# Attention scores in runs of three units and six PSUM banks instead of two units and four, in a two-layer hybrid decoder kernel

## Chip, cores, metric

One Trainium2 chip (trn2), all eight cores, one batch element on each. The metric is device time in microseconds (us) of the slowest core. A run has one of two states: fast, or slow, in which the cores of one die or of both show a lower granted TensorE clock. Only fast runs are compared. Because one die is sometimes a little disturbed within a fast run too (clock 0.99 instead of 0.998), I use a second, finer measure throughout: the mean span of the four cores of a die, taken over all dies of the timed runs whose four clocks are 0.9965 or more (my threshold; such a die counts also where the other die of its run was slow). These "undisturbed dies" of one kernel scatter by only 1.0 to 2.0 us (standard deviation), so differences of 3 us can be read from 8 to 16 of them.

## The reference

```python
for l in range(DEPTH):                                    # 2 layers
    h = h + 0.5 * g1 * swiglu(modulate(rmsnorm(h)), ffn1)  # feed-forward, width 2816
    proj = modulate(rmsnorm(h)) @ w_in                     # 1024 -> 2560: u, v, q, k, v_b
    out_a = spatial_gating(u, v, ...)
    out_b = dilated_mixture(q, k, v_b)                     # 8 heads of 64; windows (128,1), (512,4), (2048,16)
    h = h + g2 * (concat(out_a, out_b) @ w_out)
    h = h + 0.5 * g3 * swiglu(modulate(rmsnorm(h)), ffn2)
return rmsnorm(h, final_g)
# ... x is (8, 4096, 1024); a branch of the mixture works on blocks of 128 queries
# against the block before and the block itself, masked; the three branches are
# combined by their softmax denominators
```

## The kernel before

The program is recorded as tasks; a scheduler in Python gives each engine a fixed order from estimated durations and gives out the eight PSUM banks. The TensorE works through a main line (feed-forward, projections) and fits in the attention wherever its turn comes. The attention is done for two heads ("a pair") at a time: 4 pairs, 3 dilations, 8 units, so 96 units for each half of the sequence, 384 in the two layers. A unit is two blocks of queries for two heads.

```python
def scores(self, r, us, pos):               # one chain on TensorE, here for two units
    ins, banks = [], []
    for u in us:
        sb = Bank(2)                        # a unit's scores take two banks, one for each head
        banks.append(sb)
        ...
        for off, dims, ko, c, n in todo:    # 128 or 256 columns
            for h in range(2):              # head h: partitions 64*h to 64*h+63, half of the array's rows
                ...
                ins.append((lambda e, ...: e.matmul(bank(sb, h)[:, c:c + n], lhsT=ka, rhs=qa, ...),
                            [bq, bkb], 37.0 if n == 128 else 55.0))
    ins[0] = ins[0][:2] + (110.0,)
    ins[-1] = ins[-1][:2] + (110.0,)
    G.chain(ins, banks, "qk", pos=pos, extra=self.pvs[-2:-1])
    return banks

# ... then, for each unit:
#   ScalarE  exp of both banks into bf16 (gives the two banks back)
#   VectorE  times the mask
#   TensorE  up to 8 matmuls by V into one bank
#   ScalarE or VectorE  the bank added to the accumulator

def normalise(self, p, pos):                # after the last unit of a pair
    for c in range(4):
        ...                                 # ScalarE: two logarithms of 64 rows, one exp(-x) of 128
        # activation(func=AF.Ln), activation(func=AF.Ln), activation(func=AF.Exp, scale=-1.0)
        # POOL: accumulator times the result; DMA out

# feed-forward, for each of 22 column blocks and each tile of 512 tokens:
#   TensorE  8 matmuls "gate" into one bank, 8 "up" into another
#   ScalarE  tanh(gate / 2);  VectorE  (tanh + 1) * gate, gives the gate bank back
#   VectorE  times up, gives the up bank back

# the scheduler, before it takes a task for TensorE that needs n new banks:
if (t.pos > hp + 4000.0 or n > 1) and ... and sum(x <= now for x in pfree["ps"]) < self.RESERVE + n:   # RESERVE = 2
    ...                                     # not now
```

The softmax here doesn't subtract the row's maximum and nothing guards it: scores larger than these inputs give would overflow.

Of the kernel before, what the change touches and what calls it, by code (L numbers as in the profile page):

```python
# [68 lines left out]
class Graph:  # L69
# [30 lines left out]
    def _new(self, name, pos):  # L100
        t = Task()
        t.id = len(self.tasks)
        t.name = name
        t.pos = pos
        t.cur = self.M if pos is None else pos
        t.L = None
        t.wl = None
        t.main = False
        t.due = None
        t.part = None  # L110
        t.soft = ()
        t.mate = None
        t.banks, t.new = [], []
        t.nbytes, t.dma = 0, False
        t.eng = None
        t.tok = None
        t.succ = []
        self.tasks.append(t)
        return t
# [93 lines left out]

    POOLS = {"ps": 8}
    RESERVE = 2

    def schedule(self, bw=270.0, dlat=2300.0, dmargin=3000.0, cmargin=250.0, backlog=9000.0):
        pend = {e: [] for e in ENG}
# [2 lines left out]
        pfree = {p: [0.0] * n for p, n in self.POOLS.items()}  # L221
# [3 lines left out]
        order = []  # L225
        table = [None]
        pipe = [0.0]
        port = [0.0]
        for t in self.tasks:
            t.ndep = len(t.deps)  # L230
# [52 lines left out]
        def pick(e, now):  # L283

            av = avail[e]
            nxt = pend[e][0][0] if pend[e] else 1e18
            if e == "pe":
                best, bk = None, None
                while head[0] < len(mains) - 1 and mains[head[0]].eng is not None:
                    head[0] += 1  # L290
                hp = mains[head[0]].pos
                for t in av:
                    if best is not None and (t.mready <= now, -t.pos) <= bk:
                        continue
                    if t.new:
                        i, f = find_places(t.new, now)
                        if i is None:
                            nxt = min(nxt, f)
                            continue
                        n = sum(b.n for b in t.new)  # L300
                        if (t.pos > hp + 4000.0 or n > 1) and not (t.mate and t.mate.eng) and sum(x <= now for x in pfree["ps"]) < self.RESERVE + n:
                            nxt = min(nxt, max(now + 50.0, sorted(pfree["ps"])[self.RESERVE + n - 1]))
                            continue
                    best, bk = t, (t.mready <= now, -t.pos)
                return best, nxt
            best, bk = None, None
            while head[0] < len(mains) - 1 and mains[head[0]].eng is not None:
                head[0] += 1
            hp = mains[head[0]].pos
            for t in av:  # L310
                if t.new:
                    i, f = find_places(t.new, now)
                    if i is None:
                        nxt = min(nxt, f)
                        continue
                    if t.dma and (t.L > hp + 16000.0 or sum(x <= now for x in pfree[t.new[0].pool]) < 3):
                        nxt = min(nxt, now + 300.0)
                        continue
                if e != t.opts[0][0] and t.L > hp + 2500.0:
                    nxt = min(nxt, now + 300.0)  # L320
                    continue
                if not t.dma and t.mready > t.ready:
                    m = t.mready + max(0.0, min(6000.0, 0.5 * (t.L - hp - 5000.0)))
                    if m > now and t.L > hp + (m - now) + 1000.0:
                        nxt = min(nxt, max(m, now + 200.0))
                        continue
                if t.dma:
                    far = t.L - hp
                    bl = backlog if far < 12000.0 or now < 100000.0 else 5000.0 if far < 40000.0 else 2500.0
                    if pipe[0] - now > bl:  # L330
                        nxt = min(nxt, max(pipe[0] - bl, now + 50.0) if bl == backlog else now + 200.0)
                        continue
                    if pipe[0] - now > 3000.0 and any(x.dma and x.eng is None and x.L < t.L and not x.new
                                                      for x in avail["pool" if e == "sp" else "sp"]):
                        nxt = min(nxt, now + 200.0)
                        continue
                k = t.L
                if e == "dve" and port[0] > now and any(o[0] == e and o[3] == "x" for o in t.opts):
                    k += 2.0 * (port[0] - now)
                if e == "act":  # L340
                    f = next(o[3] for o in t.opts if o[0] == e)
                    if f is not None and table[0] not in TABLES[f]:
                        k += 3000.0
                if best is None or k < bk:
                    best, bk = t, k
            return best, nxt
# [4 lines left out]
        while done < total:  # L351
            cand = sorted(ENG, key=lambda e: (when[e], EI[e]))
            e = cand[0]
            now = when[e]
# [3 lines left out]
            p = pend[e]  # L358
            while p and p[0][0] <= now:
                t = heapq.heappop(p)[2]  # L360
# [3 lines left out]
            t, nxt = pick(e, now)  # L364
# [29 lines left out]
                t.ins[0] = (t.ins[0][0], t.ins[0][1] | prev) + t.ins[0][2:]  # L394
            free[e] = st + dur
            t.start, t.dur = st, dur
            if t.dma:
                pipe[0] = max(pipe[0], st + dur) + t.nbytes / bw
                t.end = pipe[0] + dlat
                t.late = max(t.end, t.mready + dur + 2000.0) + dmargin  # L400
            else:
                t.end = st + dur + LAT[e]
                t.late = max(t.end, t.mready + o[2] + LAT[e] if e != "pe" else 0.0)
# [177 lines left out]
def build_nc():  # L581
# [34 lines left out]
    with ExitStack() as st:  # L616
        arena = st.enter_context(nc.sbuf_tensor("arena", [128, AW], F32))
        ps = st.enter_context(nc.psum_tensor("ps", [128, 8, 512], F32))
# [51 lines left out]
        def steps(lo, size, n):  # L670
            return [lo + size * i for i in range(n)]
# [587 lines left out]

        BACK = {1: 128, 4: 512, 16: 2048}  # L1260

        class Attn:
            def __init__(self, half, p0, p1):
                self.half = half
                z = ACT[2]

                def at(n):
                    nonlocal z
                    z += n
                    return z - n  # L1270
                self.q = Ring([at(4096)], [128, SB], BF16, "q")
                self.k = Ring([at(8192 if half else 4096)], [128, 2 * SB if half else SB], BF16, "k")
                if half:
                    self.v = {1: Ring([at(6528)], [128, 17, 192], BF16, "v1"), 4: Ring([at(7680)], [128, 20, 192], BF16, "v4"),
                              16: Ring([at(12288)], [128, 32, 192], BF16, "v16")}
                else:
                    vv = Ring(steps(at(12288), 6144, 2), [128, 16, 192], BF16, "v")
                    self.v = {1: vv, 4: vv, 16: vv}
                self.acc0 = at(16384)
                self.pT = Ring(steps(at(6144), 2048, 3), [128, 2, 2, 2, 128], BF16, "pT")  # L1280
                self.ob = Ring(steps(at(2048), 1024, 2), [128, T], BF16, "ob")
                self.hi = z
                self.pvs = []
                units = [(p, r, u) for p in range(4) for r in (1, 4, 16) for u in range(8)]
                step = (p1 - p0) / (len(units) + 2)
                for n, (p, r, u) in enumerate(units):
                    pos = p0 + step * n
                    if r == 1 and u == 0:
                        self.start_pair(p, pos)
                    if u == 0:  # L1290
                        self.load_v(p, r, pos)
                    if u % 2 == 0:
                        banks = self.scores(r, (u, u + 1), pos)
                    self.unit(p, r, u, pos, step, banks[u % 2])
                    if r == 16 and u == 7:
                        self.normalise(p, pos + step)

# [47 lines left out]
                rho = 2 * u + b  # L1345
                return rho * 8, [[128, 16], [1, 8]], rho, bool(half), rho, 16 * half + rho

            def scores(self, r, us, pos):



# [1 line left out]
                q, k, bq, bkb = self.qa, self.ka, self.bq, self.bk  # L1353
                kb = SB if self.half else 0
                ins, banks = [], []
                for u in us:
                    sb = Bank(2)
                    banks.append(sb)
                    b0, b1 = self.blk(r, u, 0), self.blk(r, u, 1)
# [11 lines left out]
                    for off, dims, ko, c, n in todo:  # L1371
                        for h in range(2):
# [1 line left out]
                            ka = bass.AP(k.tensor, k.offset + h * 64 * k.ap[0][0] + kb + ko, [[k.ap[0][0], 64], [r, 128]])  # L1374
                            ins.append((lambda e, qa=qa, ka=ka, h=h, c=c, n=n, sb=sb: e.matmul(  # L1375
                                bank(sb, h)[:, c:c + n], lhsT=ka, rhs=qa, start=True, stop=True), [bq, bkb],
                                37.0 if n == 128 else 55.0))
                ins[0] = ins[0][:2] + (110.0,)
                ins[-1] = ins[-1][:2] + (110.0,)
                G.chain(ins, banks, "qk", pos=pos, extra=self.pvs[-2:-1])  # L1380
                return banks

# [343 lines left out]
```

## Time and profile before

| | before |
|---|---|
| first three timed runs | 4849.52, 5211.05, 5432.37 us (one fast, two slow) |
| span in the profile, slowest core | 4871.8 us |
| undisturbed dies, three chips | 4828.4, 4827.5, 4827.1 us |
| TensorE busy | 98% |
| runs of score matmuls | 192 |

The profile has these parts used below: the busy share of each engine; the chain of work that ended last; the waits (who waited for whom, us in total, times, longest); and the instructions in order of time. In the latter a row reads: start in us, duration in us, engine, source line, operation, out<-in, shape, count, and in brackets the idle time ahead of it with what ended it. Durations of matmuls are modelled and overlap; differences of starts are what to rely on. In the kernel before, L1375 are the score matmuls, L1409 those by V, L1002 gate and up, L1393 the exponential of scores, L1008 the tanh, L1436 and L1438 the logarithms, L1440 the exponential of the normalisation. In the changed kernel the same lines are L1392, L1426, L1017, L1410, L1023, L1453, L1455 and L1457.

### The profile page before, as it was taken

The page shows a single profiled execution, that of the slowest core. Times are in us where ns is not written, and L with a number is a line of the kernel's source. Part 1 is how long each engine was busy: PE and PEld are TensorE (multiplying, and loading weights), DVE is VectorE, ACT ScalarE, POOL GpSimd, SP SyncE. Part 2 cuts the span into 40 slices and gives each one's busy share as a digit, 9 for nine tenths or more (in the row PEclk, how much of TensorE's full clock was granted, in tenths as well). Part 3 has the DMA queues.
Part 4 walks back from the last instruction along what each step waited for, and adds up shares of the span by engine and source line. Part 5 has one row for each costly group of instructions (what it writes and reads, how often), then busy time and mean ns, then how long its engine had stood idle before and what let it go on. Part 6 is the DMA issues. An engine that isn't in the chain of part 4 may idle for free.

```text
span 4871.8 us, 74168 instructions; the slowest of 8 cores (4820.7 to 4871.8 us)
## 1 busy us (share of the span) xinstructions
PE 4789.6 (98%) x25859; PEld 2257.4 (46%) x25859; DVE 2461.2 (51%) x4088; ACT 2035.0 (42%) x3024; POOL 973.5 (20%) x949
## 2 busy tenths in 40 slices
PE   6999999999999999999999999999999999999998
PEld 2444445444445554444444444444444455544443
DVE  6452566473655473655233326645537544525433
ACT  5112576452755352512211127645537444525311
POOL 0001551212531111300100026312235100122101
PEclk9999999999999999999999999999999999999999
DMA  8888676777575768755721466756665644473314
GB/s 240 169 191 230 166 204 159 191 206 218 172 209 150 200 192 240 218 147 165 249 66 39 120 200 163 208 155 184 149 190 164 185 148 140 123 248 124 136 42 157
DMA packets 370033, 834.80 MB, mean 171 GB/s; under 512 B 148961, under 2 KB 182113, under 8 KB 363234
## 3 DMA queue, kind: packets, MB, share of 16 engines
q1 hardware_dynamic: 352338, 741.56, 49.4%
q0 software_dynamic: 17328, 88.49, 12.1%
q8 instruction: 213, 3.49, 0.3%
q14 instruction: 154, 1.26, 0.1%
HBM read 741.20 MB, written 234.88 MB: 200 GB/s over the span
## 4 chain that ended last, share of the span: by engine, by line
PE 92%; ACT 2%; DMA 2%; DVE 2%; issue 1%; POOL 0%; SPq 0%; DVEq 0%; ACTq 0%; POOLq 0%
PE ps L1002 48%; PE ps L1030 25%; PE ps L1141 9%; PE ps L1467 5%; PE ps L1409 3%; PE ps L1375 2%; DMA arena<-xP 1%; DMA arena<-hS 0%; DVE arena L1206 0%; DVE arena L948 0%; POOL arena L1182 0%; DMA arena<-ada_w 0%; ACT arena L1184 0%; DMA arena<-wdS 0%; PE ps L1234 0%
## 5 line engine op out<-in xcount | busy, mean ns | idle before, releaser
L1002 PE MATMUL ps<-arena 128*128 128x512 bf16 x11264 | 2511.5, 381 | 32.6 <-DMA arena<-wgu 25.0
L1002 PEld LDWEIGHTS ps<-arena 128*128 128x128 bf16 x11264 | 1083.9, 98 | 1312.0 <-issue 86.4
L1030 PE MATMUL ps<-arena 128*128 128x512 bf16 x5632 | 1242.7, 382 | 1.1 <-DMA arena<-wdS 1.1
L1008 ACT ACTIVATE arena<-ps 128x512 f32<-128x512 f32 x704 | 419.7, 597 | 1283.7 <-PE ps L1002 1279.9
L1010 DVE SCALAR_TENSOR_TENSOR arena<-arena,ps 128x512 f32<-128x512 f32 x704 | 481.4, 685 | 771.9 <-ACT arena L1008 770.7
L1030 PEld LDWEIGHTS ps<-arena 128*128 128x128 bf16 x5632 | 550.7, 98 | 665.6 <-issue 47.9
L926 POOL TENSOR_TENSOR arena<-arena 128x512 f32<-128x512 f32 (+2 forms) x351 | 414.2, 1180 | 1218.4 <-ACT arena L919 1116.3
L1034 DVE SCALAR_TENSOR_TENSOR arena<-ps,arena 128x512 f32<-128x512 f32 x256 | 192.1, 751 | 908.3 <-PE ps L1030 899.9
L1015 DVE TENSOR_TENSOR arena<-ps,arena 128x512 bf16<-128x512 f32 x704 | 485.0, 690 | 216.6 <-PE ps L1002 193.3
L1141 PE MATMUL ps<-arena 128*128 128x512 bf16 x2560 | 577.1, 385 | 9.0 <-ACT arena L1225 5.8
L919 ACT ACTIVATE arena<-arena 128x512 bf16<-128x512 f32 x424 | 250.9, 625 | 709.1 <-DVE arena L1034 379.3
L1393 ACT ACTIVATE arena<-ps 128x1024 bf16<-128x1024 f32 (+1 forms) x384 | 344.9, 950 | 308.3 <-PE ps L1375 307.6
L1141 PEld LDWEIGHTS ps<-arena 128*128 128x128 bf16 x2560 | 251.0, 99 | 314.7 <-issue 52.0
L1396 DVE TENSOR_TENSOR arena<-arena 128x1024 bf16<-128x1024 bf16 (+1 forms) x384 | 256.1, 675 | 126.0 <-ACT arena L1393 124.6
L961 ACT ACTIVATE arena<-arena 128x512 bf16<-128x512 f32 x372 | 278.4, 806 | 45.2 <-DVE arena L948 45.1
L1445 POOL TENSOR_TENSOR arena<-arena 64x512 bf16<-64x512 f32 x128 | 163.8, 1280 | 623.1 <-ACT arena L1440 600.0
L948 DVE TENSOR_TENSOR arena<-arena 128x512 f32<-128x512 f32 x384 | 268.3, 747 | 35.0 <-ACT arena L934 32.0
L1467 PE MATMUL ps<-arena 128*128 128x512 bf16 x1024 | 230.1, 386 | 0.0
L1425 DVE TENSOR_TENSOR arena<-ps,arena 128x512 f32<-128x512 f32 x256 | 175.5, 685 | 65.2 <-PE ps L1409 57.5
L1409 PEld LDWEIGHTS ps<-arena 128*128 128x128 bf16 x2736 | 173.6, 98 | 63.4 <-issue 7.1
L1213 POOL TENSOR_TENSOR arena<-arena 128x512 bf16<-128x512 f32 x128 | 167.9, 1320 | 174.8 <-DVE arena L1204 120.2
L1409 PE MATMUL ps<-arena 128*128 128x128 bf16 x2736 | 194.4, 219 | 1.9 <-DVE arena L1010 0.9
(79 smaller groups left out, 2112.7 us busy)
## 6 DMA issues: line engine op xcount, KB each, us to landing
arena<-wguS SPq DMA_DIRECT2D x242, 512.0 KB, 5.7
arena<-hS SPq DMA_DIRECT2D x204, 512.0 KB, 6.8
arena<-wdS SPq DMA_DIRECT2D x128, 704.0 KB, 5.9
arena<-ada_w SPq DMA_DIRECT2D x144, 512.0 KB, 5.9
hS<-arena SPq DMA_DIRECT2D x224, 256.0 KB, 5.8
wguS<-wgu POOLq DMA_DIRECT2D x66, 512.0 KB, 7.8
hS<-arena SPq DMA_DIRECT2D x64, 512.0 KB, 4.3
arena<-xP SPq DMA_DIRECT2D x48, 512.0 KB, 9.0
```

What stands on the lines that cost most here:

```text
L926: f = lambda e, a=a, sq=sq, out=out: e.tensor_tensor(out=out, in0=a, in1=sq, op=ALU.add)
L948: f = lambda e, hk=hk, u=u: e.tensor_tensor(out=u, in0=hk, in1=rs, op=ALU.mult)
L961: ga = act(lambda e, hk=hk, A=A, sh=sh, o=o: e.activation(out=o, in_=hk, func=AF.Identity, scale=A, bias=sh), 725)
L1002: mate = main([(lambda e, kc=kc, half=half, bk=bk, y=y, gu=gu: e.matmul(bank(bk), lhsT=gu[:, half, kc, :], rhs=y[:, kc, :], start=(kc == 0 ...
L1008: G.op([act(lambda e, sg=sg, gb=gb: e.activation(out=smv[sg.i], in_=bank(gb), func=AF.Tanh, scale=0.5), 490, "tanh")], reads=[gb], writes= ...
L1010: G.op([dve(lambda e, sg=sg, gb=gb: e.scalar_tensor_tensor(out=smv[sg.i], in0=smv[sg.i], scalar=1.0, in1=bank(gb), op0=ALU.add, op1=ALU.mu ...
L1015: G.op([dve(lambda e, sg=sg, ub=ub, o=o: e.tensor_tensor(out=o, in0=bank(ub), in1=smv[sg.i], op=ALU.mult), 610)], reads=[ub, sg], writes=[ ...
L1030: main([(lambda e, j=j: e.matmul(bank(bk), lhsT=wd[:, j, :], rhs=a[:, j, :], start=(j == 0), stop=(j == FC - 1)), [bwd, ba[j]], MM) for j ...
L1141: ins.append((lambda e, lhs=lhs, rhs=rhs, kc=kc: e.matmul(bank(bk), lhsT=lhs, rhs=rhs, start=(kc == 0), stop=(kc == KC - 1)), rd + [by[kc] ...
L1393: return e.activation(out=cut(pT, 0), in_=cut(ps[:, :, :], sb.i * 512), func=AF.Exp, scale=0.125)
L1409: return e.matmul(o, lhsT=v[:, vi, h * 64:h * 64 + 128], rhs=pT[:, h, b, pc, :], start=(pc == 0 or not prev), stop=(pc == 1))
L1467: main([(lambda e, kc=kc, m=m, bk=bk: e.matmul(bank(bk), lhsT=w[:, m, kc, :], rhs=mx[:, kc, :], start=(kc == 0), stop=(kc == KC - 1)), [bw ...
```

## The change

The intent is fewer changes between half-row and full-row matmuls: the scores of three units are issued in one run, so that there are 32 runs in a half instead of 48. The cost is that a run takes six of the eight banks.

```diff
-                    if u % 2 == 0:
-                        banks = self.scores(r, (u, u + 1), pos)
-                    self.unit(p, r, u, pos, step, banks[u % 2])
+                    if n % QKG == 0:                                   # QKG = 3
+                        banks = self.scores(units[n:n + QKG], pos)
+                    self.unit(p, r, u, pos, step, banks[n % QKG])
...
-                                37.0 if n == 128 else 55.0))
-                ins[0] = ins[0][:2] + (110.0,)
-                ins[-1] = ins[-1][:2] + (110.0,)
+                                55.0 if n == 256 else 28.0 if r < 16 else 31.0))
+                ins[0] = ins[0][:2] + (ins[0][2] + 109.0,)
+                ins[-1] = ins[-1][:2] + (ins[-1][2] + 109.0,)
...
-  ... sum(x <= now for x in pfree["ps"]) < self.RESERVE + n:
+  ... sum(x <= now for x in pfree["ps"]) < (7 if n == 6 else self.RESERVE + n):
...
+    PFAR, PLEN, PRATE = 1e9, 3000.0, 0.7
+                    if far > self.PFAR and now > 100000.0 and pace[0] - now > self.PLEN:   # never true: PFAR
+                        t.held = True
```

More of the change, by code (lines that the diff above doesn't have):

```diff
@@ L112, in _new @@
         t.mate = None
+        t.held = False
         t.banks, t.new = [], []
@@ L227, in schedule @@
         pipe = [0.0]
+        pace = [0.0]
+        pes = []
         port = [0.0]
@@ L300, in pick @@
                         n = sum(b.n for b in t.new)
-                        if (t.pos > hp + 4000.0 or n > 1) and not (t.mate and t.mate.eng) and sum(x <= now for x in pfree["ps"]) < self.RESERVE + n:
-                            nxt = min(nxt, max(now + 50.0, sorted(pfree["ps"])[self.RESERVE + n - 1]))
+                        if (t.pos > hp + 4000.0 or n > 1) and not (t.mate and t.mate.eng) and sum(x <= now for x in pfree["ps"]) < (7 if n == 6 else self.RESERVE + n):
+                            nxt = min(nxt, max(now + 50.0, sorted(pfree["ps"])[(7 if n == 6 else self.RESERVE + n) - 1]))
                             continue
@@ L331, in pick @@
                         nxt = min(nxt, max(pipe[0] - bl, now + 50.0) if bl == backlog else now + 200.0)
+                        continue
+                    if far > self.PFAR and now > 100000.0 and pace[0] - now > self.PLEN:
+                        t.held = True
+                        nxt = min(nxt, max(pace[0] - self.PLEN, now + 100.0))
                         continue
@@ L396, in schedule @@
             t.start, t.dur = st, dur
+            if e == "pe":
+                pes.append(t)
+            if t.dma and t.held:
+                x = next((x for x in reversed(pes) if x.end + 100.0 <= now), None)
+                if x is not None:
+                    t.deps = t.deps | {x}
             if t.dma:
+                pace[0] = min(max(pace[0], now) + t.nbytes / (bw * self.PRATE), max(now + 8000.0, pipe[0] + t.nbytes / bw))
                 pipe[0] = max(pipe[0], st + dur) + t.nbytes / bw
@@ L1260, in build_nc @@
         BACK = {1: 128, 4: 512, 16: 2048}
+        QKG = 3
         class Attn:
@@ L1346, in blk, with scores @@
                 return rho * 8, [[128, 16], [1, 8]], rho, bool(half), rho, 16 * half + rho
-            def scores(self, r, us, pos):
+            def scores(self, us, pos):
                 q, k, bq, bkb = self.qa, self.ka, self.bq, self.bk
@@ L1355, in scores @@
                 ins, banks = [], []
-                for u in us:
+                for _, r, u in us:
                     sb = Bank(2)
```

## The prediction

> **What bounds the kernel now.** I read the cores first, then the page's busy shares and chain, then the waits of the TensorE, then the TensorE's instructions in order of time inside an attention stage.
>
> The cores, then the page (busy time, and the chain by engine):
>
> ```profile
> core 5: 4871.8 us, clock 0.989
> die 0 (median of its cores): 4824.8 us, clock 0.998
> die 1 (median of its cores): 4864.5 us, clock 0.990
> ```
>
> ```profile
> PE 4789.6 (98%) x25859; PEld 2257.4 (46%) x25859; DVE 2461.2 (51%) x4088; ACT 2035.0 (42%) x3024; POOL 973.5 (20%) x949
> ...
> PE 92%; ACT 2%; DMA 2%; DVE 2%; issue 1%; POOL 0%; SPq 0%; DVEq 0%; ACTq 0%; POOLq 0%
> ```
>
> The profile fell in the fast state (both dies near full clock, 0.8% apart). The TensorE is busy 98% of the span and is 92% of the chain that ended last; the next engine, VectorE, is at 51%. So the span is the sum of what the TensorE streams plus what makes it stand still, and a gain must come out of that sum. The scores are one source line, L1375, two forms of 64-row matmuls (groups by form):
>
> ```profile
> L1375 PE MATMUL ps<-arena 64*128 64x128 bf16 x1792 | 117.9, 225 | 2.7 <-ACT arena L1008 1.4 <-DVE arena L1015 1.2
> L1375 PE MATMUL ps<-arena 64*128 64x256 bf16 x512 | 63.4, 269 | 0.0
> ```
>
> They lost 2.7 us to waits in the whole kernel. What they cost besides is only seen in order of time (start, duration, instructions), here 15 us of the second attention half of layer 0, the TensorE and below it ScalarE and VectorE rows of the same stretch:
>
> ```profile
> 1702.28 1.89 PE L1002 MATMUL ps<-arena 128*128 128x512 bf16 x8
> 1704.10 0.63 PE L1375 MATMUL ps<-arena 64*128 64x128 bf16 x12
> 1704.66 3.63 PE L1002 MATMUL ps<-arena 128*128 128x512 bf16 x16
> 1708.13 1.06 PE L1409 MATMUL ps<-arena 128*128 128x128 bf16 x16
> 1709.02 1.89 PE L1002 MATMUL ps<-arena 128*128 128x512 bf16 x8
> 1710.84 0.63 PE L1375 MATMUL ps<-arena 64*128 64x128 bf16 x12
> ```
>
> ```profile
> 1704.10 0.42 PEld L1375 LDWEIGHTS ps<-arena 64*128 64x128 bf16 x12 [0.42 <-issue]
> ...
> 1704.83 1.94 ACT L1393 ACTIVATE arena<-ps 128x1024 bf16<-128x1024 f32 x2
> ...
> 1705.96 0.69 DVE L1396 TENSOR_TENSOR arena<-arena 128x1024 bf16<-128x1024 bf16 x1 [0.23 <-ACT arena L1393]
> ...
> 1707.35 0.68 DVE L1396 TENSOR_TENSOR arena<-arena 128x1024 bf16<-128x1024 bf16 x1
> ```
>
> Durations here overlap, so only differences of starts count. One cycle serves two units: a run of 12 score matmuls, 16 feed-forward matmuls (L1002), 16 that multiply by V (L1409), 8 feed-forward. The 8 feed-forward matmuls ahead of the scores take 1704.10 - 1702.28 = 1.82 us; where ordinary matmuls follow, the same 8 take 1.73 (mean 1.728 over 32 places, against 1.822 over 101 places with scores behind them). So **going into a run costs 0.094 us**. The note "0.42 <-issue" says that the weight loads of the scores, which elsewhere run ahead of the matmuls, did not start earlier here.
>
> **What the Trainium skill says.** "TensorEngine Tiling (Array Packing)", Key Properties: changing the tiling mode, not just the tile, drains the TensorE. Scores contract over 64 rows and the two heads use the two halves of the array, so each run is entered and left by a mode change; the trace agrees with 0.094 us in. "TensorE: Matmul & The Clock Gate", "Wait — 56ns, not 53.3ns?": warm start to start is N / 2.4 GHz plus about 2.5 ns, 215.7 ns at N = 512. The trace agrees: 1.728 / 8 = 0.216 us. The tiling page, "Gotcha 1: PSUM Pressure": row tiles write different PSUM banks, which is why a unit takes two banks; "PSUM — Partial Sum Buffer", Specifications: there are eight. The change moves a run from four of them to six; no trace of the kernel before can show what six do.
>
> **The cost of leaving.** Start of a run to start of what follows, over runs without a wait: 0.398 us for 8 matmuls of 128 columns (32 runs), 0.648 for 16 of them (32 runs), 0.558 for 12, of which 4 have 256 columns (120 runs). The first two give 0.250 / 8 = 31 ns a matmul and a constant of 0.398 - 8 x 0.03125 = 0.148 us. For the 12, the two heads' streams of 1024 columns at the page's 2.4 GHz are 0.427 us (an estimate), which leaves 0.131. So **leaving costs 0.13 to 0.15 us**, and a run as a whole 0.094 + 0.14 = 0.235.
>
> **The change part by part.**
>
> 1. Runs. 2 layers x 2 halves x 96 units are 384 units: 192 runs of two before, 128 of three after. In the built programs the score matmuls stand in 192 runs (128 of 12, 32 of 8, 32 of 16) and in 128 (80 of 18, the others of 12, 14, 22 and 24). Each program has 2304 score matmuls, 2736 by V, and all others in equal numbers. So 64 runs go: 64 x 0.235 = 15.0 us (14.3 with 0.131, 15.5 with 0.148), and all of it lies on the TensorE, thus on the path.
>
> 2. The scores' estimates in the scheduler, and its rule that a run of six banks starts only when seven of the eight are free. They cost nothing by themselves but decide the order. With two units a run and the old estimates put back into the new file, all five engines' orders come out equal to before, so the third part of the diff, the pacing of far transfers, never acts (its threshold of 1e9 is never reached).
>
> 3. What the order makes of it. Until the first scores of each layer the TensorE's order hardly differs (8 feed-forward matmuls more ahead of them), so the start (89 us until the long feed-forward runs, over 60 of them waits for data) stays. Every run is still followed by at least 8, nearly always 16 feed-forward matmuls or a 22-matmul down chain before the first multiplication by V. After the last multiplication by V of a half, at least 340 matmuls of 512 columns (over 70 us) still stand before the output projection that needs it, in both programs. So attention stays buried in feed-forward work, and nothing waits for its end.
>
> 4. Waits. Six banks must be read out by three exponentials, each 1.94 / 2 = 0.97 us, then three maskings of 0.69. In the cycle above the exponentials would end at 1705.8, 1706.8 and 1707.7, the third masking at about 1708.04 + 0.69 = 1708.7 (the second ended at 1708.04), while the third multiplication by V would start at 1708.13 + 2 x 0.45 = 1709.03: 0.3 us of slack, an estimate from this one cycle. Two banks are left for feed-forward. The first gate chain lasts 1.73 us, and the first exponential gives two banks back about 1.2 us after the run, so the third chain finds one. But the margin is thinner than the 0.5 us of today's second unit. In the four attention stages the TensorE's waits sum to 1.7, 0.5, 1.2 and 1.6 us, 5.0 in all (the first stage, over 440 us):
>
> ```profile
> PE ps L1375 <- ACT arena L1008: 0.7, 1, 0.7
> PE ps L1375 <- DVE arena L1015: 0.5, 1, 0.5
> PE ps L1409 <- DVE arena L1010: 0.5, 1, 0.5
> ```
>
> I expect this to double or to treble: 5 us lost, with 0 to 15 possible.
>
> The sum: -15.0 + 5 = -10 us, 0.2% of the span.
>
> **The rivals.**
>
> Bank starvation: with two free banks, gate and up chains wait for exponentials, or the scores for their seven banks. For it: eight banks in all, and the rule of seven had to be made (the old rule of two in reserve would ask for eight). Against it: ScalarE is busy 229 of 410 us in the first stage and VectorE 251, and the new order keeps 16 or more feed-forward matmuls behind each run. If each of the 128 runs lost 0.5 us, that is +64 us and a net of +49, 1% slower; two waits of 0.5 would be needed in every run for 2%.
>
> No gain per run: if the drain is paid per head pair or per matmul, not per run, longer runs save nothing and the time stays at -0 to +5. Against it: 8 and 16 matmuls differ by 31 ns each, close to the 27 ns that half of 128 columns takes at 2.4 GHz, so little per-matmul cost is left to be hidden there.
>
> Gain hidden by another bound: a DMA or VectorE path sets the end. Against it: the PE share of the chain, and 0.2% is too little to uncover the next bound at 51%. It would leave 0.
>
> More banks, smoother order: fewer chain breaks could also remove today's 5 us of attention waits, for -20. I give this little.
>
> **Range and chances.** The before runs were 4849.52, 5211.05 and 5432.37 us, the latter two over 7% above the first and so slow; the prediction is for a fast run, as only such are compared. 4849.5 - 10 = 4840. The size of the effect is uncertain by -20 to +50, and fast spans differ by chip and die by some 0.5% (4871.8 in the profile with one die at 0.990, 4824.8 for the other die), so 4800 to 4890. Faster by 2% would take 97 us; all that the mode changes cost now is 192 x 0.235 = 45. So faster 0.01, within 2% 0.96, slower 0.03. Where a run falls in the slow state, it lies hundreds of us higher, for both kernels.
>
> **What would show it.** Step 1: 128 runs; 8 feed-forward matmuls ahead of one still take 1.82 us; a run of 18 takes 0.558 + 0.213 = 0.77 us, a run of 24 takes 0.148 + 24 x 0.03125 = 0.90. If 18 take 0.84 (1.5 times 0.558) the per-run cost is wrong. Step 3: starts of the first feed-forward, and the stretch from the last scores to the output projection, as before. Step 4: the TensorE's waits inside the four attention stages sum to 5 to 20 us, on L1409's and L1375's counterparts; over 20, with feed-forward waiting for ScalarE or VectorE, means the bank rival. The prediction is wrong if fast runs of the same rounds differ by over 0.6% (30 us) or the new kernel is the slower.

## The result, and the profile after

Ratios are the mean time of one kernel's fast runs over that of the other's fast runs of the same rounds, so they are not quite the ratios of the medians.

| | before | after |
|---|---|---|
| median of 6 runs, both states | 4915.72 us | 4856.27 us |
| fastest run | 4846.83 us | 4844.41 us |
| ratio of fast runs | | 1.0009 (95%: 0.9989 to 1.0029) |
| undisturbed dies, same chip and rounds (run again later) | 4827.1 us (14 dies) | 4826.3 us (8 dies) |

The time did not move: the medians differ only because more of before's runs were slow, and on undisturbed dies the difference is 0.8 us, where 10 had been forecast.

The cores, the busy shares and the chain of the changed kernel:

```profile
core 5: 4853.0 us, clock 0.993
die 0 (median of its cores): 4826.7 us, clock 0.998
die 1 (median of its cores): 4846.7 us, clock 0.993
```

```profile
PE 4762.0 (98%) x25859; PEld 2254.9 (46%) x25859; DVE 2465.2 (51%) x4088; ACT 2041.4 (42%) x3025; POOL 978.2 (20%) x952
...
PE 93%; ACT 2%; DMA 2%; issue 1%; DVE 1%; POOL 0%; SPq 0%; DVEq 0%; ACTq 0%; POOLq 0%
```

The span of the page is 19 us shorter than before's 4871.8, but that is core 5, on die 1, at clock 0.993 instead of 0.989. Die 0, undisturbed in both, went from 4824.8 to 4826.7. The TensorE is the bound as before.

**An account of the TensorE.** To see where the forecast gain went I summed up the TensorE's rows of the trace after the first 600 us: from each row's start to the next one's, less the wait noted at the next, less 0.2159 us for each matmul of 512 columns and 0.0558 for each of 128. What is left ahead of the scores is the cost of going in (with any standing that no wait names). Means of three undisturbed cores before (1 to 3) and six after, in us:

| term | before | after (second profile) | difference |
|---|---|---|---|
| the runs of scores, start to what follows | 105.0 | 96.6 | -8.4 |
| remainder ahead of runs | 19.0 | 14.4 | -4.6 |
| waits that the trace names | 18.1 | 28.8 | +10.7 |
| remainder elsewhere | 7.2 | 8.9 | +1.7 |
| sum | 149.3 | 148.7 | -0.6 |

So the saving is there, 13.0 us, and waits and unnamed standing take 12.4 of it back. Where? "Losses" below are the named waits around the attention, plus standing of over 0.1 us ahead of a run and named waits within the 12 rows that follow it. They went from 7.7 to 17.3 us a core, and those that fall **at the first run of a pair of heads** from 3.1 to 13.0. That is 0.8 us on average over the 16 pairs (from 0 to 2.3); the other runs lose 4.3 us in all, where it was 4.6 before. Here are two such places, core 1. Before, the TensorE and ScalarE rows:

```profile
788.18 0.62 PE L1375 MATMUL ps<-arena 64*128 64x128 bf16 x12
788.73 5.35 PE L1002 MATMUL ps<-arena 128*128 128x512 bf16 x24
...
787.01 1.28 ACT L1436 ACT_TABLE_LOAD   x1
788.31 0.63 ACT L1436 ACTIVATE arena<-arena 64x512 f32<-64x512 f32 x1
788.95 1.28 ACT L1008 ACT_TABLE_LOAD   x1
790.25 0.60 ACT L1008 ACTIVATE arena<-ps 128x512 f32<-128x512 f32 x1
790.74 1.94 ACT L1393 ACTIVATE arena<-ps 128x1024 bf16<-128x1024 f32 x2
```

And after:

```profile
778.72 21.52 PE L1017 MATMUL ps<-arena 128*128 128x512 bf16 x96
800.37 0.84 PE L1392 MATMUL ps<-arena 64*128 64x128 bf16 x18
801.14 1.90 PE L1017 MATMUL ps<-arena 128*128 128x512 bf16 x8
804.04 1.89 PE L1017 MATMUL ps<-arena 128*128 128x512 bf16 x8 [1.00 <-DVE arena L1025]
...
798.44 1.28 ACT L1453 ACT_TABLE_LOAD   x1
799.74 0.63 ACT L1453 ACTIVATE arena<-arena 64x512 f32<-64x512 f32 x1
800.46 0.63 ACT L1455 ACTIVATE arena<-arena 64x512 f32<-64x512 f32 x1
801.10 1.28 ACT L1023 ACT_TABLE_LOAD   x1
802.40 0.60 ACT L1023 ACTIVATE arena<-ps 128x512 f32<-128x512 f32 x1
802.89 2.85 ACT L1410 ACTIVATE arena<-ps 128x1024 bf16<-128x1024 f32 x3
```

In both, ScalarE is not ready when the scores are: it is in the normalisation of the pair before, with a table load to the logarithm and one back. The exponentials start equally late, 790.74 - 788.18 = 2.56 us after the run's start before and 802.89 - 800.37 = 2.52 after. Before, 24 feed-forward matmuls (three banks) go by without a wait, as a run leaves four banks. There ScalarE is held from 787.01 to 790.25, 3.24 us. After, it is held from 798.44 to 802.40, 3.96 us. The first 8 feed-forward matmuls fit in; the next 8 need a bank that waits for a tanh at 802.40 and then for VectorE (L1025), and the TensorE stands for 1.00 us. The run of 96 matmuls ahead also shows standing that no wait names: 800.37 - 778.72 = 21.65 us, where 96 x 0.2159 and 0.094 for going in make 20.82. (With 1.00 + 0.83 us this is one of the dearer places.)

That is a theory so far: **the six banks leave the TensorE two, and at the start of each pair ScalarE, held up by table loads, gives banks back too late (A)**. Rivals: any burst of three exponentials is too long for two banks, wherever it comes (A2); the scheduler's new estimates made a worse order by themselves; or the saving read from the starts isn't real on the path.

### The profile page after: what moved, and what is told of

Its sections match the earlier page's. It is cut to its first block, busy times and chain, and to the rows that moved or that the text cites. A ratio compares the mean times of both kernels' runs of the same rounds, so it can differ in the third digit from the quotient of the medians.

```text
span 4853.0 us, 74112 instructions; the slowest of 8 cores (4822.7 to 4853.0 us)
## 1 busy us (share of the span) xinstructions
PE 4762.0 (98%) x25859; PEld 2254.9 (46%) x25859; DVE 2465.2 (51%) x4088; ACT 2041.4 (42%) x3025; POOL 978.2 (20%) x952
## 4 chain that ended last, share of the span: by engine, by line
PE 93%; ACT 2%; DMA 2%; issue 1%; DVE 1%; POOL 0%; SPq 0%; DVEq 0%; ACTq 0%; POOLq 0%
PE ps L1017 48%; PE ps L1045 25%; PE ps L1156 10%; PE ps L1484 5%; PE ps L1426 3%; PE ps L1392 2%; DMA arena<-xP 1%; ACT arena L1023 0%; DVE arena L1221 0%; DMA arena<-wguS 0%; POOL arena L1197 0%; DMA arena<-hS 0%; DMA arena<-ada_w 0%; PE ps L1249 0%; ACT L1453 0%
## 5 line engine op out<-in xcount | busy, mean ns | idle before, releaser
L1025 DVE SCALAR_TENSOR_TENSOR arena<-arena,ps 128x512 f32<-128x512 f32 x704 | 482.0, 686 | 803.7 <-ACT arena L1023 802.6
L1413 DVE TENSOR_TENSOR arena<-arena 128x1024 bf16<-128x1024 bf16 (+1 forms) x384 | 255.2, 683 | 97.4 <-ACT arena L1410 95.7
L1442 DVE TENSOR_TENSOR arena<-ps,arena 128x512 f32<-128x512 f32 x256 | 175.9, 687 | 60.3 <-PE ps L1426 53.9
```

The lines of the kernel that those rows point to most:

```text
L1025: G.op([dve(lambda e, sg=sg, gb=gb: e.scalar_tensor_tensor(out=smv[sg.i], in0=smv[sg.i], scalar=1.0, in1=bank(gb), op0=ALU.add, op1=ALU.mu ...
```

## The experiments

Twelve kernels ran, in three groups; the kernels of a group shared chip and runs of before. The accounts (us a core, undisturbed cores of the profile with all records) in one table; the experiments follow.

| kernel | runs | scores and remainder ahead | losses | of them first run of a pair | undisturbed dies | before, same rounds |
|---|---|---|---|---|---|---|
| before | 192 | 124.0 | 7.7 | 3.1 | | 4827 to 4828 |
| changed (e12) | 128 | 111.0 | 17.3 | 13.0 | 4826.3 | 4827.1 |
| e1 two units, new estimates | 192 | 123.9 | 7.6 | 2.4 | 4828.1 | 4828.4 |
| e2 one unit | 344 | 160.7 | 10.2 | (runs merge, not told apart) | 4867.5 | 4828.4 |
| e3 three, no logarithm | 128 | 109.3 | 3.6 | 2.7 | 4810.6 | 4828.4 |
| e4 first run of two | 144 | 113.0 | 12.8 | 6.7 | 4823.2 | 4828.4 |
| e5 two, no logarithm | 192 | 123.1 | 2.5 | 2.0 | 4820.8 | 4827.5 |
| e6 two, six banks | 192 | 124.4 | 15.8 | 7.0 | 4853.9 (fast runs, clock 0.995 up) | 4827.5 |
| e7 runs of 2,2,2,3,... | 144 | 112.4 | 10.2 | 2.8 | 4822.1 | 4827.5 |
| e8 logarithms joined | 128 | 109.7 | 19.8 | 14.8 | 4831.5 | 4827.5 |
| e9 three, after normalisation | 128 | 109.2 | 4.6 | 2.6 | 4810.0 | 4827.1 |
| e10 two, after normalisation | 192 | 123.3 | 3.2 | 2.7 | 4820.6 | 4827.1 |
| e11 rule of eight | 128 | | | | 5613.5 (fast runs) | 4827.1 |

### e1: the new estimates alone

```diff
-        QKG = 3
+        QKG = 2
```

> Two units a run again, but with the scheduler's new estimates for the scores: the part of the change that only reorders. Theory A (the longer runs save about 12 us of mode changes and their six banks bring about 11 us of new TensorE waits): this kernel has the 192 runs and the four banks of before, so its score runs plus entries sum to 123 us as before, its losses in the attention to about 8 us, and its time equals before within 0.1%. Rival (the new estimates alone make the order worse, whatever the banks): 8 to 12 us slower than before, ratio 1.002.

Measured: ratio 1.0016 (0.998 to 1.0052; one of the six runs had a die at clock 0.988), undisturbed dies 4828.1 against 4828.4; 192 runs, losses 7.6. The estimates and the reordering that comes of them are worth nothing either way. That rival falls.

### e2: one unit a run

```diff
-        QKG = 3
+        QKG = 1
```

> One unit a run: the program has 344 runs of scores instead of 192. If going in and out costs 0.22 us a run, as the traces of before and after give (0.094 in, 0.13 out), the score runs and their entries take 152 x 0.22 = 34 us more than before, 157 us in all, and the time is 30 to 36 us longer (ratio 1.006 to 1.0075), less up to 5 us of today's waits, as a run takes two banks only. If the saving per run that I read from the starts is not real on the path, the ratio is 1.000 to 1.002.

Measured: ratio 1.0086 (1.0071 to 1.01), dies 4867.5, 39.1 us above before. The score runs took 126.1 us and the remainder ahead of them 34.6; less before's 124.0 that is 36.7 us for 152 runs, 0.24 us each. The time rose slightly more than the range I gave, by the losses (10.2 instead of 7.7), which I had expected to shrink. So the price of a run is real and lies on the path, in the size that the starts gave.

### e3 and e5: the same orders without the logarithm's table

```diff
-  e.activation(out=rc()[0:64, :], in_=acc[64:128, c, 0, :], func=AF.Ln)
+  e.activation(out=rc()[0:64, :], in_=acc[64:128, c, 0, :], func=AF.Identity, scale=0.015)
```

(and the same for the other half; e5 with two units and the old estimates besides). Their outputs are wrong, which doesn't matter for the times. The scheduler is still told "ln", so no instruction moves; only the table loads around the logarithms go.

> The changed kernel in exactly its order, but the logarithms in the normalisation that ends each pair of heads are replaced by a scaled copy, which needs no other activation table: wrong result on purpose, and no instruction added or moved. Theory A1 (ScalarE is held up at the start of each pair of heads by the table loads of the pair before, 1.28 us each, so the exponentials give the six banks back late): the losses at the first run of a pair fall from 13 us to under 5 us a core, all attention losses from 18 to under 9, and the time is 8 to 12 us below the changed kernel's, so ratio 0.998 against before. Rival A2 (any burst of three exponentials is too long for the two banks that are left): the losses stay at 15 us or more and the time stays.

> The kernel before in exactly its order, with the logarithms of the normalisation replaced by the scaled copy (wrong on purpose), so without their table loads. Theory (longer runs save 12 us; their banks need ScalarE at the start of a pair, which the table loads hold up): the losses fall from 8 to about 3 us a core, so the time is 4 to 6 us below before (ratio 0.999), and the three-unit kernel without logarithms, 17 us below before, stays 11 to 13 us better than this one: the gain of the longer runs without their cost. Rival (the table loads cost both kernels the same 14 us or more, and the longer runs gain nothing even without them): this one is 14 to 17 us below before too.

Measured: e3 ratio 0.9964 (0.9942 to 0.9985), dies 17.8 us below before; e5 ratio 0.9983 (0.9957 to 1.0008), 6.7 us below before. The same place in e3, core 1:

```profile
773.67 20.88 PE L1017 MATMUL ps<-arena 128*128 128x512 bf16 x96
794.48 0.84 PE L1392 MATMUL ps<-arena 64*128 64x128 bf16 x18
795.25 3.63 PE L1017 MATMUL ps<-arena 128*128 128x512 bf16 x16
...
794.65 0.60 ACT L1023 ACTIVATE arena<-ps 128x512 f32<-128x512 f32 x1 [0.91 <-PE ps L1017]
795.42 2.86 ACT L1410 ACTIVATE arena<-ps 128x1024 bf16<-128x1024 f32 x3 [0.18 <-PE ps L1392]
```

ScalarE is idle when the scores come, the three exponentials start 0.94 us after the run's start, and 16 feed-forward matmuls follow without a wait. The 96 ahead take 20.81 us, the 20.82 worked out above: the unnamed standing is gone too. The time fell by more than the 8 to 12 us that I had expected, as the losses that the kernel before has too went with the rest. The losses fell from 17.3 to 3.6 us in an unchanged order of instructions, so bursts of three exponentials are not too long for two banks as such: A2 falls. And without the hold-up three units beat two by 11 us (e3 lies 17.8 us below before's dies, e5 6.7), as large as the gain that had been expected at first.

### e4 and e7: short runs where ScalarE is held up

```diff
-        QKG = 3
+        GROUPS = (2, 3, 3, 3, 3, 3, 3, 2, 2)          # e7: (2, 2, 2, 3, 3, 3, 3, 3, 3)
...
-                    if n % QKG == 0:
+                    if n % 24 in STARTS:              # a run starts where a group starts
```

> Runs of 2, 3, 3, 3, 3, 3, 3, 2, 2 units in each pair of heads: 144 runs, so the first run of a pair, where the changed kernel loses 13 of its 18 us, takes four banks. Theory A: mode changes save 48 x 0.22 = 10.5 us, losses go back to 8 to 10 us a core, the time is 8 to 10 us below before (ratio 0.998). Rival A2 (six banks lose wherever they are taken): the losses stay at 15 us or more and the ratio is 1.000 to 1.002.

> Runs of 2, 2, 2, 3, 3, 3, 3, 3, 3 units in a pair of heads: 144 runs as in the kernel with the first run of two, but the six units nearest to the last pair's normalisation all go in runs of four banks. Theory: 48 x 0.21 = 10 us of mode changes saved, losses 7 to 9 us a core as before (mean 7.7), time 9 to 11 us below before, ratio 0.998, and 3 to 6 us below the kernel whose first run alone is short. Rival (six banks also lose later in the pair once they come first there): losses of 12 or more.

Measured: e4 ratio 1.0018 (0.9974 to 1.0061, with one run that had a disturbed die), dies 5.2 us below before, losses 12.8, of them 6.7 at first runs. e7 ratio 0.998 (0.995 to 1.001), dies 5.4 us below, losses 10.2. Both miss the forecast: the first run of a pair does better with four banks (13.0 to 6.7 and to 2.8), but some of the loss goes to later runs, in e7 2.6 us to the fifth, the second of the long ones. Of the 11.0 and 11.6 us that the mode changes save, about half is still lost. In e4 the losses account for it (5.1 us above before's); in e7 they are only 2.5 us above, and the other 4.0 are waits and standing elsewhere that I did not trace. A cheap cure by group sizes works only in part.

The loss of e7's fifth run falls on 3 of the 16 pairs (0.4, 0.4 and 1.8 us on every core read). At each a table load stands between the run and its first exponential, which starts 1.94 us late; at the first two it is the load back from the logarithm of an RMS norm (L947), not of the attention's normalisation. So any table load in front of a run of three can cost.

### e6: six banks for two units

```diff
+                self.spare = Bank(2)
-                G.chain(ins, banks, "qk", ...)
+                G.chain(ins, banks + [self.spare], "qk", ...)       # never written
...
-   reads=[bC["mk"]], ... name="mask"
+   reads=[bC["mk"]] + ([self.spare] if last else []), ... name="mask"   # given back here
```

> Two units a run and before's estimates, but each run also takes a third pair of banks, which nothing writes and which is given back when the second masking ends, about where a third exponential would end; the rule of seven free banks then holds as in the changed kernel. If the number of banks left is what costs (two beside the run): 192 runs and their 123 us as before, losses of 15 us or more with the first runs of a pair at 10 or more, time 8 to 15 us above before (ratio 1.002 to 1.003). If the burst of three exponentials is what costs (more work for ScalarE between two runs): losses stay at 8 to 10 and the ratio within 0.001 of 1.

Measured: ratio 1.0048 (1.0026 to 1.007), 26 us above before, more than either forecast. Losses around the attention are 15.8, as the bank theory says, but only 7.0 of them at first runs. The rest of the time is lost elsewhere: with 192 runs that each ask for seven free banks the attention gets done later, the built order of layer 0 ends it 112 matmuls ahead of the output projection in one half and 66 in the other, where it had been 340 or more, and that projection then waits for its data (waits of the TensorE, core 1):

```profile
PE ps L1485 <- DMA arena<-mS: 6.7, 1, 6.7
```

So this shows that taking six banks costs by itself, also without a third exponential. The total can't be parted into bank count and lateness here, but the loss at a run can (see the table after e8).

### e8: fewer table loads, longer blocks

```diff
-  two tasks, one activation(func=AF.Ln) each
+  one task that issues both, so nothing comes between them
```

> The changed kernel with the two logarithms of a quarter recorded as one task, so that nothing comes between them: in the built order ScalarE changes to the logarithm's table 32 times instead of 50. Correct result. Theory A1: fewer table loads (about 18 to the logarithm and as many back, 36 x 1.28 = 46 us of ScalarE), so the losses at the first run of a pair fall from 13 to 6 to 10 us a core, and the time is 3 to 8 us below before. Rival (what counts is the length of the ScalarE block, not the number of loads; a joined block of 1.28 + 1.25 us holds the exponentials up just as long): losses stay at 13 and the time at before's.

Measured: ratio 0.9997 (0.9959 to 1.0035), dies 4.0 us above before, losses 19.8, of them 14.8 at first runs. (The profile: die 1 at 0.98; the account and the rows are of die 0, at 0.998.) The rival that I had set against theory A here is right: the number of loads isn't what counts. The place, core 1:

```profile
784.98 1.90 PE L1017 MATMUL ps<-arena 128*128 128x512 bf16 x8
789.00 1.89 PE L1017 MATMUL ps<-arena 128*128 128x512 bf16 x8 [2.13 <-DVE arena L1025]
...
782.30 1.28 ACT L1454 ACT_TABLE_LOAD   x1
...
786.18 1.28 ACT L1023 ACT_TABLE_LOAD   x1
787.47 0.60 ACT L1023 ACTIVATE arena<-ps 128x512 f32<-128x512 f32 x1
```

From 782.30 to 787.47 ScalarE takes nothing out of PSUM, 5.2 us instead of 4.0, and the wait is 2.13 us instead of 1.00. What counts, then, is how long ScalarE is away while only two banks are left. One place would be thin ground for that, so here is a count over all runs of the traces. How late ScalarE comes is taken as the time from the start of a run of scores to its first exponential. Each cell has the mean loss of a run and, in brackets, the number of such runs a core (before: 3 cores; the others: 6; of e6 without the last two runs of a pair, where the waits ahead of the output projection fall):

| first exponential after | before: two units, four banks | changed (e12): three units, six banks | e6: two units, six banks |
|---|---|---|---|
| under 1.5 us | 0.03 us (170) | 0.02 us (112) | 0.01 us (154) |
| 1.5 to 2 us | 0.11 us (9) | 0.30 us (7) | 0.90 us (2.2) |
| 2 to 2.5 us | 0.10 us (6) | 0.98 us (5.3) | 1.02 us (2.3) |
| over 2.5 us | 0.16 us (7) | 1.79 us (4) | 1.88 us (2) |

In the kernel before, with four banks, a late ScalarE costs little. With six the loss grows with the delay, and from 2 us on e6, which has no third exponential, loses as much a run as the changed kernel. Its first runs lose less in sum (7.0 against 13.0 us) because fewer of them come 2 us late or more: 4.3 of 16 a core against 7.3. The runs of two in e4 are less clear: they lost 0.42 us at 1.5 to 2 us (3.3 runs a core), nothing at 2 to 2.5, and 0.8 us where ScalarE came over 3.5 us late (2 runs a core).

### e9 and e10: the first run waits for the normalisation

```diff
+                self.recs = []                        # in normalise: the four exponentials are kept here
...
-                G.chain(ins, banks, "qk", pos=pos, extra=self.pvs[-2:-1])
+                G.chain(ins, banks, "qk", pos=pos, extra=self.pvs[-2:-1] + self.recs)
+                self.recs = []
```

> The changed kernel, but the first run of scores of a pair of heads is made to wait for the last exponential of the normalisation of the pair before, so it takes its six banks only when ScalarE is done with logarithms; the TensorE does feed-forward matmuls meanwhile, which the built order shows (still 128 runs; ScalarE's changes to the logarithm's table fall from 50 to 19 on the way). Correct result. Theory (the loss is ScalarE held up by the normalisation while two banks are left): losses at the first run of a pair under 5 us a core, all losses under 9, mode changes as in the changed kernel, time 10 to 15 us below both kernels (ratio 0.997 to 0.998). Rival (the later start makes the end of the attention late, or six banks lose anyway): losses 12 or more, or new waits ahead of the output projection, ratio 0.999 or more.

> The same wait for the normalisation, in the kernel before (two units a run). Theory: its losses at the first three runs of a pair (6.6 of 7.7 us) shrink to about 3, time 3 to 6 us below before, ratio 0.999; so three units with this wait stay 8 to 12 us better than two units with it. If most of the gain of the three-unit kernel with the wait came from the wait itself, this one gains 10 us or more too.

Measured: e9 is correct and its undisturbed dies lie 17.1 us below before's and 16.3 below the changed kernel's; e10's lie 6.5 below before's. The ratios of fast runs, 0.9941 (0.9874 to 1.0009) and 0.9956 (0.9873 to 1.0039), lean on one run of before at 4887.52 us, so I rely on the dies. e9, core 1:

```profile
796.69 0.84 PE L1393 MATMUL ps<-arena 64*128 64x128 bf16 x18
797.46 3.63 PE L1017 MATMUL ps<-arena 128*128 128x512 bf16 x16
...
780.44 1.28 ACT L1455 ACT_TABLE_LOAD   x1 [0.47 <-DVE arena L1444]
781.73 2.18 ACT L1455 ACTIVATE arena<-arena 64x512 f32<-64x512 f32 x4
783.94 2.19 ACT L1457 ACTIVATE arena<-arena 64x512 f32<-64x512 f32 x4
786.15 2.19 ACT L1460 ACTIVATE arena<-arena 128x512 f32<-128x512 f32 x4
788.36 1.28 ACT L1023 ACT_TABLE_LOAD   x1
```

The scheduler now puts all eight logarithms and four exponentials of a pair between one table load and the next, 9.2 us in one piece, and no run of scores holds banks meanwhile. (In this kernel L1393 are the scores, L1455 and L1457 the logarithms, L1460 the exponential of the normalisation.) Table loads to the logarithm fell from 50 to 19 a core. Losses are 4.6, the saving of the mode changes 14.8. Three units with the wait beat two units with it by 10.6 us. (e9 by itself does not part the wait from the fewer table loads; but e8 had fewer loads too, without the wait, and its losses did not fall.)

### e11: ask for all eight banks

```diff
-  (7 if n == 6 else self.RESERVE + n)
+  (8 if n == 6 else self.RESERVE + n)
```

> The changed kernel with a run of six banks starting only when, by the scheduler's estimate, all eight are free, instead of seven. If the missing eighth bank at the start is the cause, losses fall under 9 us a core and the time by 8 or more. Theory (two free banks are used up 3.5 us after the run begins, and a ScalarE held up by 3.8 us of logarithms and table loads comes later than that, eighth bank or not): losses at the first run of a pair stay at 8 us or more and the time within 6 us of the changed kernel's.

Measured: ratio 1.1597 (1.15 to 1.1694), about 5613 us. Neither forecast comes near. The scheduler did not find eight banks free while feed-forward work was running, so attention was put off and stands alone: in the trace (core 0) all 128 runs of scores are followed directly by multiplications by V, with no feed-forward between (waits of the TensorE, slowest core):

```profile
PE ps L1426 <- DVE arena L1413: 338.6, 213, 5.2
PE ps L1392 <- DVE arena L1442: 98.3, 81, 2.9
```

The matmuls by V wait for the masks of their own units (L1413), the scores for additions to the accumulator (L1442). The built order shows this too. The run says nothing on the eighth bank; it says how sharp the rule of seven is.

### e12: the changed kernel again

> The changed kernel itself once more, on the same chip and in the same rounds as the three others, so that they can be compared without a change of chip. Its undisturbed dies should again give the mean of before's within 2 us (4827 to 4829), mode changes 12 us less than before and losses about 10 us more.

Measured: dies 4826.3 against 4827.1; scores and remainder ahead 13.0 us less than before, losses 17.3. The result holds on the chip of e9 to e11. (The ratio, 0.997, has a range of 0.9856 to 1.0084 with two fast runs only.)

## Why the prediction was wrong

The time lay in the range given, but the range was 90 us wide, so that says little; the change that was forecast, -10 us, did not come.

- Step 1, the saving: right, at its low end. A run of 18 took 0.778 us (0.77 forecast), one of 24 took 0.898 (0.90), and the 8 matmuls ahead still took 1.82. Score runs fell by 8.4 us, 0.131 a run, the lower of the two figures for leaving. Going in fell by 64 x 0.094 = 6.0, of which 4.6 is left in the account as some runs stand ahead of their scores unnamed; so 14.4 instead of 15.0 with the going in at its full 6.0, and 13.0 in the account. (The prediction's 14.3 for the lower figure is 14.4 by its own terms.) e2 and the pairs e3/e5 and e9/e10 (mode changes 13.8 and 14.1 us apart) confirm it.
- Step 2, the estimates cost nothing: right (e1).
- Step 3, the attention stays buried in feed-forward work: right; in the traces of both kernels (core 1) at least 352 matmuls of 512 columns stand before the output projection. Its "over 60 us" of waits in the first 89 us is a misreading: the trace names 42. Nothing rests on it, as the start is the same in both.
- **Step 4, the waits: this failed.** It put +5 us, from "this one cycle", at 1702 to 1709 us in the middle of a pair, where ScalarE is free when the scores come and the third exponential has slack. That holds for most runs: the 112 that are not the first of a pair lose 4.3 us in all. The trace has another cycle at the start of a pair, where ScalarE can still be away on the logarithms and table loads of the pair before, 4 us at the place shown; the 16 first runs lose 13.0 us, 0.8 on average. The step's term was +5, with 15 as its upper end; it measured 13.8 (10.7 in named waits, 1.7 elsewhere, 1.4 unnamed ahead of runs), against the 14.4 saved.
- The rival of bank starvation had the right mechanism and the wrong argument against it: "ScalarE is busy 229 of 410 us" is a mean over a stage. Its size, 0.5 us in each of 128 runs, was wrong too: it is 0.8 in 16.
- The check "waits inside the four attention stages sum to 5 to 20" was met (14.4 on core 1, 5.1 before, over the windows 690 to 1100, 1410 to 1840, 3065 to 3470 and 3785 to 4215 us) and so could not have told a good forecast from a bad one.

What is not settled: where e7 loses the 4.0 us outside the attention, and how the time that e6 adds is shared between its banks and its later order.

## What to carry to other kernels

When a change makes a burst hold more of a shared buffer, look for the moment at which the engine that empties the buffer is away longest, and set the burst's hold against that moment rather than against a typical cycle or the engine's mean load. If the rare moment is known (here the normalisation with its table loads), order the burst behind it: one added dependency turned a gain of zero into 17 us (0.35%). And with effects of a few us in 4800, compare undisturbed dies and sums of trace rows, as the times of whole runs could not have told any of this.

## What the Trainium skill lacked or had wrong

- "TensorEngine Tiling (Array Packing)", Key Properties, says that a change of tiling mode drains the TensorE, but not what it costs. Here going into a run of scores took 0.094 us and coming out 0.13 us, and e2 measured 0.24 us a run.
- No page that I found says how a hold of many PSUM banks meets a busy reader. Here: a run that leaves two of eight banks lost 1.0 us where the reading engine began 2 to 2.5 us after it, 1.8 us where later, and 0.02 us where it began within 1.5 us; before's runs, which leave four, lost 0.10 to 0.16 us on average at the same delays.
- "ScalarE: Activation LUTs", Terms, gives about 2.7 us for a table load, and its section "What ACT_TABLE_LOAD costs" makes that up of 1283 ns for the load and about 1380 ns of DRAIN. Here every ACT_TABLE_LOAD took 1283 ns, as "ScalarE activation tables: per-element evaluation and per-set limits", section "What a function is on this engine", has it, and no such drain is seen: in e9 the load at 788.36 begins 0.02 us after the exponentials end, and the logarithm begins 1.29 us after the load at 780.44.
- "TensorE: Matmul & The Clock Gate", Part 1, "Seeing it yourself", tells an all-core kernel to budget a clock of 13/16 for sustained dense matmul. In the fast runs here (e11 apart), with dense matmuls on all eight cores, the mean granted clock of a core was 0.985 or more, 0.998 on undisturbed dies. The level 13/16 = 0.81 does occur, but in slow runs and for a time: in the slow profile of e8, cores 4 and 5 stood at 0.81 from 100 to 600 us and cores 6 and 7 from 4500 us to the end, and all four at 1.00 from 1000 to 2000 us.
